# A list schedule with durations from the trace and a lock for the port that DVE and POOL share, and one count moved from ACT to DVE

## The chip, the cores and the metric

The kernel runs on one core of one Trainium2 chip. The metric is the device time of one execution in microseconds (us); the kernel before takes 649.95 us in the median of three runs (649.72 to 651.6). The engines are PE (TensorE, matrix products), DVE (VectorE), ACT (ScalarE), POOL (GpSimd) and SP, which here only issues DMAs. Each engine works through its own queue strictly in order, and an instruction that waits holds up everything behind it on its engine.

## The reference

One layer of a hybrid trunk on a sequence of 1024 tokens and 1024 channels:

```
h = rmsnorm(x, norm_g);  z = h @ w_in              # one projection, split into 14 parts
A: causal pooling over windows 2, 4, 8, 16, per-group map, scale, gated by silu(pg)
B: score = sum_h iw_h * relu(iq_h . ik)            # 8 indexer heads of 32
   sel   = top_k(score where admissible, 256)      # per query; admissible: chunks of 64 keys
   attention of 6 heads over the selected keys, gated by silu(dg)
C: softmax(q.k/8 + F[t] - F[s], s <= t) @ v, F = cumsum(log_sigmoid(ff + bias)); 6 heads, silu(fg)
x = x + concat(A, B, C) @ w_out;  return rmsnorm(x, final_g)
```

## The kernel before

Each product is made of three passes in a 32-bit matmul format (high part by high part, high by low, low by high), so a projection tile is 24 matmuls (8 slices of the inner dimension, 3 passes) into one PSUM bank. Banks 0, 1 and 6 hold projections (tag `pj`), 2 and 3 scores (`s`), 4 and 5 transposes (`pt`), 6 and 7 attention outputs. A bank that is full is read twice, first by ACT (the high part, or the tanh of a gate), then by DVE (the low part, or the gate itself); only then may PE write it again.

The program is recorded first and ordered afterwards. Every operation is put down with its engine, a planned duration, what it reads and writes, and a priority (lines 111 to 142). `schedule` (line 161) then plays the program in planned time: over all engines it takes the operation that can start earliest, by priority where several can within 3 ns, and gives out the buffers in that order. The instructions are emitted in the order of the planned starts. So the planned durations (`t_act`, `t_dve`, `t_pool`, `t_mm`, lines 275 to 288) are in no instruction, but they decide the order on every queue.

In order of the program: normalization of 8 token tiles (lines 497 to 527; the one-column chain on DVE and POOL is lines 481 to 490) and the indexer's projection (462, 544 to 567); the indexer's scores of tiles 2 to 7 (line 595 the products, 599 ACT's relu, 603 and 607 the weighted sum on DVE); the channel projections of keys, queries, values and gates, with weights split on ACT and POOL (438, 439, 694, 695); the search for the 256th largest score; attention C, attention B (919 to 1008); the output projection (1122 to 1160).

The search (lines 757 to 797) finds the threshold of each query bit by bit, 32 rounds of counting for the six tiles 2 to 7 at once (tile i has (i+1)*128 columns). In a round each tile's scores are compared with the threshold and counted: tiles 5, 6, 7 by ACT (line 771, 768, 896 and 1024 columns), tiles 2, 3, 4 by DVE (line 776, 384, 512 and 640). Then DVE makes the next threshold by lines 790 (needs only the threshold), 792 (needs all six counts) and 793, on six columns; the next round starts after 793. There are 31 such decisions after the first. `finish` (lines 799 to 850) makes masks of the thresholds on DVE, starting with line 805; a tile counted by ACT takes one more count (819) and six one-column steps (826 to 834). Beside the search run the value projections (evicted by ACT 664 and DVE 665), the pool mixer (DVE 1073 to 1085, PE 1081) and the first gates of attention C (ACT 736, DVE 738, a buffer `th` of which there are two, which the pool mixer uses as well).

Of the kernel before, what the change touches and what calls it, by code (L numbers as in the profile page):

```python
# [76 lines left out]
class Op:  # L77
    __slots__ = ("eng", "fn", "dur", "pr", "seq", "deps", "bufs", "outs", "end", "left", "bytes", "lag", "tr")


class Plan:
# [29 lines left out]
    def op(self, eng, fn, dur, r=(), w=(), pr=0.0, nbytes=0, lag=0.0, tr=False):  # L111
        o = Op()
        o.eng, o.fn, o.dur, o.pr, o.seq, o.bytes, o.lag = eng, fn, dur, pr, self.seq, nbytes, lag
        o.tr = tr
        self.seq += 1
        deps, bufs = set(), set()
        for k in r:
            bufs.add(k[0] if isinstance(k, tuple) else k)
            if k in self.last_w:
                deps.add(self.last_w[k])  # L120
        for k in w:
            bufs.add(k[0] if isinstance(k, tuple) else k)
            if k in self.last_w:
                deps.add(self.last_w[k])
            deps.update(self.readers.get(k, ()))
        for k in r:
            self.readers.setdefault(k, []).append(o)
        for k in w:
            self.last_w[k] = o
            self.readers[k] = []  # L130
        deps.discard(o)
        o.deps = deps
        o.bufs = [b for b in bufs if isinstance(b, Buf)]
        for b in o.bufs:
            b.left += 1
        o.outs = []
        o.left = len(deps)
        o.end = None
        for d in deps:
            d.outs.append(o)  # L140
        self.ops.append(o)
        return o
# [20 lines left out]
    def schedule(self):  # L163
# [9 lines left out]
        was_tr = False  # L173
        while len(order) < n:
            best = None
            for e, lst in ready.items():
                cand = []
                tmin = None
                for o in lst:
                    t = free[e] + (0.085 if e == PE and was_tr and not o.tr else 0.0)  # L180
                    for d in o.deps:
                        if d.eng == e:
                            x = d.end if e in (SP, PE, ACT) else d.end + 0.13
                        else:
                            x = d.end + self.LAT[d.eng] + (self.SLACK if e == PE else 0.0) + o.lag
                        if x > t:
                            t = x
                    ok = True
# [33 lines left out]
            if e == PE:  # L222
                was_tr = o.tr
            if e == SP:
# [50 lines left out]
def t_act(n, psum=False, acc=False):  # L275
    return (0.052 if psum else 0.094) + n / 1200.0 + (0.093 if acc else 0.0)
# [10 lines left out]
def t_mm(n):  # L287
    return 0.07 if n < 0 else max(n * 0.41667e-3 + 0.003, 0.107)
# [3 lines left out]
def tile_trunk(ctx: ExitStack, tc: tile.TileContext, x, w_in, norm_g, pool_w, pool_scale,  # L292
# [76 lines left out]
    V = lambda fn, n, r, w, pr=0.0, two=False, acc=False, fast=1: P.op(DVE, fn, t_dve(n, two, acc, fast), r, w, pr)  # L369
    G = lambda fn, n, r, w, pr=0.0: P.op(POOL, fn, t_pool(n), r, w, pr)  # L370
# [107 lines left out]
    def rstd(ss, k_ss, pr, two=False):  # L478
# [7 lines left out]
        P.op(POOL, lambda: nc.gpsimd.tensor_tensor(r0(), v(), half(), op=OP.pow), 0.47, [(b, 0), k_half], [(b, 1)], pr)  # L486
# [63 lines left out]
    def rep(i, h0, n, pr):  # L550
# [5 lines left out]
            .to_broadcast([128, n, 4, 32])), n * 189 + 10, [Z[i]], [zt], pr)  # L556
# [193 lines left out]
    def search(tiles, on_act):  # L750
# [14 lines left out]
        def count(t, kt):  # L765
            for c, i in sorted(enumerate(tiles), key=lambda x: x[1] not in on_act):
                n = (i + 1) * 128
                s = (lambda: 0.0) if t is None else (lambda c=c: t()[:, c:c + 1])
                if i in on_act:
                    jk = P.new("jka", [128, n], BF)  # L770
                    A(lambda c=c, i=i, jk=jk, s=s: nc.scalar.activation(jk(), SC[i](), AF.Sign, bias=s(), scale=-1.0,  # L771
                                                                         accum_out=cn()[:, c:c + 1]), n,
                      sck(i) + kt, [jk, k("cn", c)], pr, acc=True)
# [115 lines left out]
    def unit(kind, pair, g, ks, VV):  # L889
# [6 lines left out]
        for hd in range(2):  # L896
# [11 lines left out]
            for j in range(3, -1, -1):  # L908
                t = 4 * g + j
                Ps.insert(0, [])  # L910
                for u in range(g + 1):
# [13 lines left out]
                    if dg:  # L925
# [8 lines left out]
                      [Pt, (mx, j, u)], pr, two=True)  # L934
# [106 lines left out]
    def pool_tile(m, consts):  # L1041
# [13 lines left out]
        def add(dst, src, sh, r0, r1):  # L1055
            ksrc = kv if src is v else [(src, "d"), (src, "z")]
            G(lambda: nc.gpsimd.tensor_tensor(dst()[r0:r1, 16:], src()[r0:r1, 16:], src()[r0:r1, 16 - sh:W - sh],
                                              op=OP.add), 1024, ksrc, [(dst, "d")], pr)

        def cp():  # L1060
            G(lambda: nc.gpsimd.tensor_copy(s2()[0:64, 16:], s1()[0:64, 16:]), 1600, [(s1, "d")], [(s2, "d")], pr)
# [129 lines left out]
    on_act = [5, 6, 7]  # L1191
    tiles = on_act + [2, 3, 4]
# [46 lines left out]
```

## Time and profile before

| | |
|---|---|
| median of three runs | 649.95 us |
| profiled execution: its own time, its span | 651.98 us, 650.2 us |
| PE, DVE, ACT, POOL busy | 627.8, 474.4, 425.5, 201.6 us |
| granted PE clock, mean | 0.992 of full speed |
| DMA queue of SP | 102 MB, 55.3% of 16 engines' span |

Busy times are unions of an engine's instructions in the trace. The rows of a timeline give the start in us from the beginning of the span, the time taken, the engine, the line of the kernel, the operation, what it writes and reads, and how many instructions are merged; in brackets stands the engine's idle time before it and what ended it. A matmul's end is modelled, so a busy PE is read by its starts: in the stretch 600 to 630 us, 134 matmuls fill 30.00 us.

### The profile page before, as it was taken

The page shows a single profiled execution, that of the slowest core. Times are in us where ns is not written, and L with a number is a line of the kernel's source. Part 1 is how long each engine was busy: PE and PEld are TensorE (multiplying, and loading weights), DVE is VectorE, ACT ScalarE, POOL GpSimd, SP SyncE. Part 2 cuts the span into 40 slices and gives each one's busy share as a digit, 9 for nine tenths or more (in the row PEclk, how much of TensorE's full clock was granted, in tenths as well). Part 3 has the DMA queues.
Part 4 walks back from the last instruction along what each step waited for, and adds up shares of the span by engine and source line. Part 5 has one row for each costly group of instructions (what it writes and reads, how often), then busy time and mean ns, then how long its engine had stood idle before and what let it go on. Part 6 is the DMA issues. An engine that isn't in the chain of part 4 may idle for free. (4 is left out here: it accounts for less than half of the span.)

```text
span 650.2 us, 10279 instructions
## 1 busy us (share of the span) xinstructions
PE 627.8 (97%) x3280; PEld 529.0 (81%) x3280; DVE 474.4 (73%) x1187; ACT 425.5 (65%) x945; POOL 201.6 (31%) x218
## 2 busy tenths in 40 slices
PE   8799999999999999799999999999999999999995
PEld 7698777789988999588888888888888687788884
DVE  5987999877776887889997768766757877643322
ACT  6645678698899888513478776688477879622121
POOL 3510212450017640126252614312131625232211
PEclk9999999999999999989999999999999999999999
DMA  8616453461026337845669678599946554547311
GB/s 241 192 53 176 148 156 109 129 184 44 0 87 157 103 127 208 196 124 138 176 200 247 202 211 212 155 252 270 242 162 169 166 165 148 157 161 226 120 43 66
DMA packets 95380, 102.72 MB, mean 158 GB/s; under 512 B 8055, under 2 KB 64471, under 8 KB 95326
## 3 DMA queue, kind: packets, MB, share of 16 engines
q1 hardware_dynamic: 95326, 102.07, 55.3%
q8 instruction: 26, 0.43, 0.3%
q14 instruction: 28, 0.23, 0.1%
HBM read 72.09 MB, written 29.96 MB: 157 GB/s over the span
## 5 line engine op out<-in xcount | busy, mean ns | idle before, releaser
L462 PE MATMUL bank<-RA 128*128 128x512 f32 (+2 forms) x2016 | 481.4, 378 | 3.8 <-DVE FA L738 3.8
L462 PEld LDWEIGHTS bank<-RA 128*128 128x128 f32 x2016 | 359.7, 189 | 54.0 <-DVE FA L738 4.3
L771 ACT ACTIVATE FA<-FA 128x768 bf16<-128x768 f32 (+2 forms) x96 | 99.6, 1037 | 15.8 <-DVE FA L793 12.4
L695 POOL TENSOR_TENSOR RA<-FA,RA 128x512 fp32r<-128x512 f32 x44 | 60.2, 1382 | 145.7 <-ACT RA L694 129.4
L941 ACT ACTIVATE FA<-FA 128x512 f32<-128x512 f32 (+3 forms) x144 | 86.8, 605 | 19.2 <-DVE FA L936 19.0
L963 ACT ACTIVATE RA<-bank 128x512 fp32r<-128x512 f32 (+1 forms) x120 | 64.5, 552 | 41.5 <-PE bank L956 36.7
L930 DVE CUSTOM_DVE_ANT_0 FA<-bank,FA 128x512 f32<-128x512 f32 (+3 forms) x144 | 77.3, 550 | 19.6 <-PE bank L922 11.2
L965 DVE TENSOR_TENSOR RA<-bank,RA 128x512 fp32r<-128x512 f32 (+1 forms) x120 | 74.1, 634 | 20.2 <-ACT RA L963 18.5
L956 PE MATMUL bank<-FA 128*128 128x128 f32 x432 | 72.6, 275 | 1.0 <-ACT FA L941 1.0
L776 DVE TENSOR_SCALAR_CACHE_REDUCE FA<-FA 128x384 bf16<-128x384 f32 (+2 forms) x96 | 71.2, 742 | 1.9
L956 PEld LDWEIGHTS bank<-FA 128*128 128x128 f32 x432 | 53.6, 140 | 20.9 <-ACT FA L941 4.3
L607 DVE SCALAR_TENSOR_TENSOR FA<-FA 128x512 f32<-128x512 f32 (+3 forms) x70 | 52.8, 776 | 2.3
L919 PE MATMUL bank<-RA 128*128 128x512 f32 (+3 forms) x144 | 52.1, 362 | 0.3 <-DVE FA L930 0.2
L974 PE MATMUL bank<-RA 128*128 128x512 f32 (+3 forms) x144 | 50.1, 376 | 0.5 <-DVE RA L965 0.5
L922 PE MATMUL bank<-RA 128*128 128x512 f32 (+3 forms) x144 | 50.1, 352 | 0.0
L599 ACT ACTIVATE FA<-bank 128x512 f32<-128x512 f32 (+3 forms) x80 | 39.7, 527 | 15.1 <-PE bank L595 6.2
L926 POOL TENSOR_TENSOR FA<-FA 128x128 f32<-128x128 f32 x48 | 29.1, 610 | 65.4 <-DVE FA L930 45.5
L969 PE MATMUL bank<-RA 128*128 128x512 f32 (+3 forms) x144 | 45.4, 341 | 0.3 <-DVE FA L1003 0.3
L1123 POOL TENSOR_TENSOR RA<-FA,RA 128x1024 fp32r<-128x1024 f32 x8 | 19.2, 2399 | 46.4 <-ACT RA L1122 35.3
L1135 DVE TENSOR_TENSOR FA<-bank,FA 128x512 f32<-128x512 f32 x16 | 11.0, 687 | 30.9 <-PE bank L462 30.9
L1007 POOL TENSOR_TENSOR FA<-FA 128x512 f32<-128x512 f32 x12 | 16.1, 1348 | 56.0 <-DVE FA L1003 35.9
L919 PEld LDWEIGHTS bank<-RA 128*128 128x128 f32 x144 | 27.1, 188 | 6.2 <-DVE FA L930 2.5
(145 smaller groups left out, 689.1 us busy)
## 6 DMA issues: line engine op xcount, KB each, us to landing
FA<-in_w_in_dram SPq DMA_DIRECT2D x60, 256.0 KB, 3.8
FA<-in_x_dram SPq DMA_DIRECT2D x15, 512.0 KB, 4.1
RA<-qk_fq SPq DMA_DIRECT2D x12, 512.0 KB, 8.2
RA<-qk_dq SPq DMA_DIRECT2D x12, 512.0 KB, 11.2
RA<-qk_dk SPq DMA_DIRECT2D x18, 256.0 KB, 6.0
mix<-FA SPq DMA_DIRECT2D x16, 256.0 KB, 4.1
FA<-in_w_out_dram SPq DMA_DIRECT2D x16, 256.0 KB
FA<-mix SPq DMA_DIRECT2D x8, 512.0 KB
```

The source lines that it names most:

```text
L462: M(lambda: nc.tensor.matmul(p()[:, :n], fa(), fb(), start=st, stop=sp), n, keys, [p], pr)
L607: V(lambda rl=rl, w=w, acc=acc, wc=wc: nc.vector.scalar_tensor_tensor(acc(), rl()[:, :w], wc(), acc(), op0=OP.mult, op1=OP.add), w, [rl, ( ...
L695: G(lambda raw=raw, s=s: nc.gpsimd.tensor_tensor(Wl()[:, s, :], raw(), f32(Wh()[:, s, :]), op=OP.subtract), 512, [raw, (Wh, kh)], [(Wl, kh ...
L771: A(lambda c=c, i=i, jk=jk, s=s: nc.scalar.activation(jk(), SC[i](), AF.Sign, bias=s(), scale=-1.0, accum_out=cn()[:, c:c + 1]), n, sck(i) ...
L776: V(lambda c=c, i=i, jk=jk, s=s: nc.vector.tensor_scalar(jk(), SC[i](), s(), None, op0=OP.is_lt, op1=OP.add, accum_out=cn()[:, c:c + 1]), ...
L919: M(lambda s=s, k=k, n=n, j=j, hd=hd: nc.tensor.matmul(s()[:, :n], q()[:, hd, j * 128:j * 128 + 128], k()[:, hd, :n], start=True, stop=False),
L922: M(lambda s=s, k=k, n=n, j=j, hd=hd: nc.tensor.matmul(s()[:, :n], q()[:, 2 + hd, j * 128:j * 128 + 128], k()[:, hd, :n], start=False, sto ...
L930: V(lambda s=s, Pt=Pt, n=n, u=u, j=j, mx=mx, bias=bias: nc.vector.tensor_tensor_reduce(Pt()[:, :n], s()[:, :n], bias()[:, u * 512:u * 512 ...
L941: A(lambda Pt=Ps[j][u], n=n, j=j, u=u, hd=hd, nm=nm: nc.scalar.activation(Pt()[:, :n], Pt()[:, :n], AF.Exp, bias=nm()[:, j:j + 1], accum_o ...
L956: M(lambda pt=pt, j=j, d=d, Pt=Ps[j][kb // 4], c=kb % 4 * 128: nc.tensor.transpose(pt()[:, j * 128 - d:j * 128 - d + 128], Pt()[:, c:c + 1 ...
L963: A(lambda ph=ph, pt=pt, c=c: nc.scalar.activation(ph()[:, c], pt()[:, c], AF.Copy), n, [pt], [ph], pr, psum=True)
L965: V(lambda ph=ph, pl=pl, pt=pt, c=c: nc.vector.tensor_tensor(pl()[:, c], pt()[:, c], f32(ph()[:, c]), op=OP.subtract), n, [pt, ph], [pl], pr)
```

## The change

Three things are changed, and nothing else. First, planned durations: an accumulating ACT operation is planned 0.1 us longer (a count of the search 0.12 us more on top), a matmul 0.0105 us longer, a transpose 0.0025 us shorter, POOL's replication, additions and copy of the pool mixer shorter (lines 561, 1063, 1066 of the new kernel), its power 0.03 us longer, and attention's masked maximum (line 936 before) without the surcharge for two inputs. Second, the planner knows a lock: an operation marked `lock` is not planned to start while another marked one runs. Marked are the DVE operations recorded with `two` or `fast`, and POOL's operations recorded through `G` with more than four columns. Third, tile 5 is counted by DVE in place of ACT.

```
+                    if o.lock:
+                        t = max(t, port)
...
+            if o.lock:
+                port = t + o.dur
...
-    return (0.052 if psum else 0.094) + n / 1200.0 + (0.093 if acc else 0.0)
+    return (0.052 if psum else 0.094) + n / 1200.0 + (0.193 if acc else 0.0)
...
-    return 0.07 if n < 0 else max(n * 0.41667e-3 + 0.003, 0.107)
+    return 0.0675 if n < 0 else max(n * 0.41667e-3 + 0.0135, 0.107)
...
-    V = lambda fn, n, r, w, pr=0.0, two=False, acc=False, fast=1: P.op(DVE, fn, t_dve(n, two, acc, fast), r, w, pr)
-    G = lambda fn, n, r, w, pr=0.0: P.op(POOL, fn, t_pool(n), r, w, pr)
+    V = lambda fn, n, r, w, pr=0.0, two=False, acc=False, fast=1: P.op(DVE, fn, t_dve(n, two, acc, fast), r, w, pr,
+                                                                       lock=two or fast > 1)
+    G = lambda fn, n, r, w, pr=0.0: P.op(POOL, fn, t_pool(n), r, w, pr, lock=n > 4)
...
-                    A(lambda c=c, i=i, jk=jk, s=s: nc.scalar.activation(jk(), SC[i](), AF.Sign, bias=s(), scale=-1.0,
-                                                                         accum_out=cn()[:, c:c + 1]), n,
-                      sck(i) + kt, [jk, k("cn", c)], pr, acc=True)
+                    P.op(ACT, lambda c=c, i=i, jk=jk, s=s: nc.scalar.activation(jk(), SC[i](), AF.Sign, bias=s(), scale=-1.0,
+                                                                         accum_out=cn()[:, c:c + 1]), t_act(n, acc=True) + 0.12,
+                      sck(i) + kt, [jk, k("cn", c)], pr)
...
-                      [Pt, (mx, j, u)], pr, two=True)
+                      [Pt, (mx, j, u)], pr)
...
-    on_act = [5, 6, 7]
-    tiles = on_act + [2, 3, 4]
+    on_act = [6, 7]
+    tiles = on_act + [2, 3, 4, 5]
```

The lines of the new kernel lie up to 5 higher than those of the kernel before (776 is 781, 792 is 797, 793 is 798, 738 is 743, 736 is 741, 1081 is 1086, 919 is 924). Three places show what the new plan moves.

DVE at the end of the search, before: the last round's counts (776), the two decision steps, the first step of `finish` (805) and a step of the pool mixer (1085).

```order
L793 SCALAR_TENSOR_TENSOR FA<-FA 128x6
L776 TENSOR_SCALAR FA<-FA 128x384
L790 TENSOR_SCALAR FA<-FA 128x6
L776 TENSOR_SCALAR FA<-FA 128x512
L776 TENSOR_SCALAR FA<-FA 128x640
L1085 SCALAR_TENSOR_TENSOR FA<-bank_67,FA 128x512
L792 TENSOR_TENSOR FA<-FA 128x6
L793 SCALAR_TENSOR_TENSOR FA<-FA 128x6
L805 TENSOR_SCALAR FA<-FA 128x3
L1085 SCALAR_TENSOR_TENSOR FA<-bank_67,FA 128x512
```

The same place in the changed kernel:

```order
L798 SCALAR_TENSOR_TENSOR FA<-FA 128x6
L781 TENSOR_SCALAR FA<-FA 128x384
L795 TENSOR_SCALAR FA<-FA 128x6
L781 TENSOR_SCALAR FA<-FA 128x512
L781 TENSOR_SCALAR FA<-FA 128x640
L781 TENSOR_SCALAR FA<-FA 128x768
L797 TENSOR_TENSOR FA<-FA 128x6
L798 SCALAR_TENSOR_TENSOR FA<-FA 128x6
L743 SCALAR_TENSOR_TENSOR FA<-FA,bank_65 128x512
L810 TENSOR_SCALAR FA<-FA 128x2
```

A round has a fourth count of 768 columns, the pool mixer's steps have gone forward (they stand two rounds earlier), and the first gate's step on bank 0 (`bank_65`) follows the last decision at once.

PE where the pool mixer's second pair of products meets the gates of attention C, before (`bank_65`, `bank_66`, `bank_71` are the projection banks 0, 1 and 6, `bank_67` and `bank_68` the score banks):

```order
L462 MATMUL bank_65<-RA 128x512 x24
L462 MATMUL bank_66<-RA 128x512 x24
L919 MATMUL bank_68<-RA 128x512
L922 MATMUL bank_68<-RA 128x512
L462 MATMUL bank_71<-RA 128x512 x7
L1081 MATMUL bank_67<-FA 128x512
L462 MATMUL bank_71<-RA 128x512 x6
L1081 MATMUL bank_67<-FA 128x512
L462 MATMUL bank_71<-RA 128x512 x5
L919 MATMUL bank_67<-RA 128x384
L922 MATMUL bank_67<-RA 128x384
L462 MATMUL bank_71<-RA 128x512 x6
```

And now, to the fourth gate tile:

```order
L467 MATMUL bank_65<-RA 128x512 x12
L1086 MATMUL bank_67<-FA 128x512
L1086 MATMUL bank_68<-FA 128x512
L467 MATMUL bank_65<-RA 128x512 x12
L467 MATMUL bank_71<-RA 128x512 x8
L924 MATMUL bank_67<-RA 128x512
L927 MATMUL bank_67<-RA 128x512
L924 MATMUL bank_68<-RA 128x384
L927 MATMUL bank_68<-RA 128x384
L467 MATMUL bank_71<-RA 128x512 x16
L467 MATMUL bank_66<-RA 128x512 x24
L467 MATMUL bank_65<-RA 128x512 x24
```

The pair of products now goes into two banks and stands in the first gate tile instead of the third. In both programs the fourth gate tile (the next 24 into `bank_65`) comes after the same matmuls.

ACT at the end of the search, before:

```order
L771 ACTIVATE FA<-FA 128x768
L771 ACTIVATE FA<-FA 128x896
L771 ACTIVATE FA<-FA 128x1024
L736 ACTIVATE FA<-bank_65 128x512
L736 ACTIVATE FA<-bank_66 128x512
```

And now:

```order
L776 ACTIVATE FA<-FA 128x896
L776 ACTIVATE FA<-FA 128x1024
L776 ACTIVATE FA<-FA 128x896
L776 ACTIVATE FA<-FA 128x1024
L699 ACTIVATE RA<-FA 128x512
L741 ACTIVATE FA<-bank_65 128x512
```

The count of 768 columns is gone from each round; the first gate of attention C is still read behind the last count of the search.

## Rows read from the trace of the kernel before

**Rows 1.** The page, busy us (share of the span) and instructions.
```profile
PE 627.8 (97%) x3280; PEld 529.0 (81%) x3280; DVE 474.4 (73%) x1187; ACT 425.5 (65%) x945; POOL 201.6 (31%) x218
```

**Rows 2.** What PE waited for: us in total, times, longest us.
```profile
PE bank L462 <- DVE FA L738: 3.8, 1, 3.8
PE bank L522 <- DVE RA L527: 2.3, 2, 1.2
PE bank L595 <- ACT FA L599: 2.2, 3, 0.8
```

**Rows 3.** Timeline in the scores, from 72 us.
```profile
72.11 3.77 POOL L695 TENSOR_TENSOR RA<-FA,RA 128x512 fp32r<-128x512 f32 x2 [7.61 <-ACT RA L694]
72.30 4.79 DVE L607 SCALAR_TENSOR_TENSOR FA<-FA 128x512 f32<-128x512 f32 x4
...
77.17 0.33 PE L595 MATMUL bank<-RA 128*128 128x128 f32 x1 [0.73 <-ACT FA L599]
...
77.62 0.73 DVE L607 SCALAR_TENSOR_TENSOR FA<-FA 128x512 f32<-128x512 f32 x1
```

**Rows 4.** Timeline of an undisturbed round of the search, DVE alone.
```profile
256.17 0.17 DVE L793 SCALAR_TENSOR_TENSOR FA<-FA 128x6 int32<-128x6 int32 x1
256.37 0.61 DVE L776 TENSOR_SCALAR_CACHE_REDUCE FA<-FA 128x384 bf16<-128x384 f32 x1
...
257.82 0.88 DVE L776 TENSOR_SCALAR_CACHE_REDUCE FA<-FA 128x640 bf16<-128x640 f32 x1
...
259.94 0.17 DVE L792 TENSOR_TENSOR FA<-FA 128x6 int32<-128x6 f32 x1 [1.23 <-ACT FA L771]
260.14 0.17 DVE L793 SCALAR_TENSOR_TENSOR FA<-FA 128x6 int32<-128x6 int32 x1
```

**Rows 5.** Groups by form: count, busy us, mean ns, idle us before.
```profile
L771 ACT ACTIVATE FA<-FA 128x768 bf16<-128x768 f32 x32 | 29.8, 932 | 12.8 <-DVE FA L793 12.4 <-DVE FA L785 0.2
...
L790 DVE TENSOR_SCALAR FA<-FA 128x6 int32<-128x6 int32 x31 | 13.3, 428 | 0.0
...
L738 DVE SCALAR_TENSOR_TENSOR FA<-FA,bank 128x512 f32<-128x512 f32 x16 | 10.9, 682 | 6.6 <-ACT FA L736 6.5
...
L665 DVE TENSOR_TENSOR RA<-bank,RA 128x384 fp32r<-128x384 f32 x16 | 8.9, 555 | 3.4 <-ACT RA L664 3.3
...
L792 DVE TENSOR_TENSOR FA<-FA 128x6 int32<-128x6 f32 x31 | 7.9, 255 | 22.8 <-ACT FA L771 22.6
...
L1085 DVE SCALAR_TENSOR_TENSOR FA<-bank,FA 128x512 f32<-128x512 f32 x4 | 3.0, 748 | 0.4 <-PE bank L1081 0.4
...
L1073 DVE SCALAR_TENSOR_TENSOR FA<-FA 128x1024 f32<-128x1024 f32 x2 | 2.6, 1278 | 0.0
...
L819 DVE TENSOR_SCALAR_CACHE_REDUCE FA<-FA 128x768 bf16<-128x768 f32 x2 | 2.0, 1009 | 0.0
```

**Rows 6.** Line 793: ns min/median/max, first and last start.
```profile
L793 DVE SCALAR_TENSOR_TENSOR FA<-FA x31: 160/167/172, 133.3 to 268.5; 128x6 int32<-128x6 int32 x31
```

**Rows 7.** Timeline at 210 us, POOL and DVE.
```profile
210.10 1.29 POOL L439 TENSOR_TENSOR RA<-FA,RA 128x512 fp32r<-128x512 f32 x1
210.11 1.30 DVE L792 TENSOR_TENSOR FA<-FA 128x6 int32<-128x6 f32 x1 [2.47 <-ACT FA L771]
```

**Rows 8.** Timeline where the search ends and PE waits.
```profile
268.71 0.17 DVE L805 TENSOR_SCALAR FA<-FA 128x3 int32<-128x3 int32 x1
...
273.56 1.23 ACT L736 ACTIVATE FA<-bank 128x512 f32<-128x512 f32 x2 [5.29 <-DMA mix<-FA]
...
275.26 0.68 DVE L738 SCALAR_TENSOR_TENSOR FA<-FA,bank 128x512 f32<-128x512 f32 x1
...
275.99 15.32 PE L462 MATMUL bank<-RA 128*128 128x512 f32 x54 [3.82 <-DVE FA L738]
```

**Rows 9.** Busy time of each engine by stretch (PE, PEld, DVE, ACT, POOL), clock, DMA.
```profile
250.00:300.00 50.00, 45.57 (x191) 36.37 (x190) 42.65 (x107) 24.11 (x48) 13.23 (x11) 0.93 0.66 171
600.00:630.00 30.00, 30.00 (x134) 24.85 (x133) 9.11 (x20) 5.42 (x9) 8.71 (x6) 1.00 0.24 88
```

More of the change, by code (lines that the diff above doesn't have):

```diff
@@ L77 @@
 class Op:
-    __slots__ = ("eng", "fn", "dur", "pr", "seq", "deps", "bufs", "outs", "end", "left", "bytes", "lag", "tr")
+    __slots__ = ("eng", "fn", "dur", "pr", "seq", "deps", "bufs", "outs", "end", "left", "bytes", "lag", "tr", "lock")
 class Plan:
@@ L109, in new, with op @@
         return b
-    def op(self, eng, fn, dur, r=(), w=(), pr=0.0, nbytes=0, lag=0.0, tr=False):
+    def op(self, eng, fn, dur, r=(), w=(), pr=0.0, nbytes=0, lag=0.0, tr=False, lock=False):
         o = Op()
         o.eng, o.fn, o.dur, o.pr, o.seq, o.bytes, o.lag = eng, fn, dur, pr, self.seq, nbytes, lag
-        o.tr = tr
+        o.tr, o.lock = tr, lock
         self.seq += 1
@@ L172, in schedule @@
         n = len(self.ops)
-        was_tr = False
+        was_tr, port = False, 0.0
         while len(order) < n:
@@ L485, in rstd @@
               k_ss[1:] + [(b, 0)], [(b, 0)], pr, two=True)
-        P.op(POOL, lambda: nc.gpsimd.tensor_tensor(r0(), v(), half(), op=OP.pow), 0.47, [(b, 0), k_half], [(b, 1)], pr)
+        P.op(POOL, lambda: nc.gpsimd.tensor_tensor(r0(), v(), half(), op=OP.pow), 0.5, [(b, 0), k_half], [(b, 1)], pr)
         V(lambda: nc.vector.scalar_tensor_tensor(a(), r0(), r0(), v(), op0=OP.mult, op1=OP.mult), 1,
@@ L555, in rep @@
             Z[i]()[:, 32 * (h0 - z0):32 * (h0 - z0 + n)].rearrange("p (h b) -> p h b", b=32)[:, :, None, :]
-            .to_broadcast([128, n, 4, 32])), n * 189 + 10, [Z[i]], [zt], pr)
+            .to_broadcast([128, n, 4, 32])), 61 * n, [Z[i]], [zt], pr)
         return zt
@@ L1057, in add @@
             G(lambda: nc.gpsimd.tensor_tensor(dst()[r0:r1, 16:], src()[r0:r1, 16:], src()[r0:r1, 16 - sh:W - sh],
-                                              op=OP.add), 1024, ksrc, [(dst, "d")], pr)
+                                              op=OP.add), 800, ksrc, [(dst, "d")], pr)
         def cp():
-            G(lambda: nc.gpsimd.tensor_copy(s2()[0:64, 16:], s1()[0:64, 16:]), 1600, [(s1, "d")], [(s2, "d")], pr)
+            G(lambda: nc.gpsimd.tensor_copy(s2()[0:64, 16:], s1()[0:64, 16:]), 412, [(s1, "d")], [(s2, "d")], pr)
         add(s1, v, 1, 0, 128)
```

## The prediction

> **What bounds the kernel now.** I read the busy times first: PE is busy for 97% of the span, DVE for 73%, ACT for 65% [rows 1]. So the time is PE's own work plus the gaps in it, and a change of order can win or lose only gaps. In full flow 134 matmuls fill 30.00 us [rows 9], 0.224 us each, and nothing in the diff changes the number of matmuls. Next I read what PE waited for. One wait stands out, 3.8 us for line 738; the transposes of the normalization (522) cost 2.3, the indexer's products (595) 2.2 in three waits [rows 2]. The timeline at the large one shows its chain: ACT cannot read the first gate tile until a buffer is free (it waits 5.29 us for the pool mixer's store), DVE finishes bank 0 at 275.26 + 0.68, and PE starts the fourth gate tile at 275.99 after 3.82 us idle, so it had arrived at 272.2 [rows 8]. [...] That place is worth 3.8 + 3 = 6.8 us, and it depends on when the search ends. So the search is what I work out.
>
> **The search, step by step.** Before, a round is set by ACT: three counts, and DVE idles 1.23 us of an undisturbed round for them; from decision to decision it lasts 260.14 - 256.17 = 3.97 us [rows 4]. The change takes 32 counts of 0.93 us from ACT and gives DVE 32 of 1.01 us (by the same kind of count in line 819) [rows 5]. DVE's new round: the first three counts run from 256.37 to 257.82 + 0.88 = 258.70, that is 2.33; the fourth adds 1.01 and some 0.05 between them; line 792 to 793 is 0.20, 793 to the next count 0.20, and some 0.05 in front of 792 [rows 4]. Sum 3.84, I take 3.85. ACT's two remaining counts are far below that. So an undisturbed round is hardly shorter: 3.85 against 3.97.
>
> What changes is what else hides in it. Before, other DVE work fell into the 1.23 us of idleness; now it adds to the round. Between the first decision and the last the new order has on DVE 2 low parts of line 723 (0.68, as 738), 16 of 665 (0.555), 4 of 738 (0.682), 4 of 1085 (0.748), 2 of 1073 (1.278) and 4 steps of 16 columns (0.17, taken as a step of six) [rows 4, 5]: 1.4 + 8.9 + 2.7 + 3.0 + 2.6 + 0.7 = 19.3. Neighbours on DVE overlap a little (the accumulator's read-out, about 0.08 each), 28 x 0.08 = 2.2 off: 17.1.
>
> The third part is the port. In the row at 210.11 the decision step 792, six columns, takes 1.30 us instead of 0.17, exactly beside a POOL subtraction of 1.29 [rows 7]. Summed: 790 takes 13.3 us for 31 and 792 takes 7.9 [rows 5]; at 0.17 each they would take 5.3 and 5.3, so the excess is 8.0 + 2.6 = 10.6. Before, the 8.0 at line 790 lay mostly within DVE's idle time. In the new round it lies on the chain. [...]
>
> I charge 9 of the 10.6, since in the first three rounds ACT, with weight splits in its queue, still sets the pace. Bounds: 4 (half of the collisions happen to fall beside counts) and 16 (each of the two steps hit one and a half times as often, as POOL has more work in the denser stretch).
>
> The start: the first decision was at 133.3 [rows 6]. In the new order the indexer's scores end slightly later in PE's queue, but they should run smoother: four steps of line 607 took 4.79 us next to two POOL subtractions of 3.77, where a step alone takes 0.73, and PE waited 0.73 for it [rows 3]. These are operations the lock does cover. Of the 2.2 us at line 595 [rows 2] I take 1.0 as won (bounds: 2.2 won, 2.2 lost in new waits) and put the first decision at 132.3. This gain is not added again: PE loses it at the gate if the search is late.
>
> Last decision: 132.3 + 30 x 3.85 + 17.1 + 9 = 273.9, against 268.5 [rows 6]. Now the first gate's DVE step stands right behind it and ACT's part is done by then (two counts and 1.2 us, less than a round), so bank 0 is free at 273.9 + 0.17 + 0.68 = 274.8. The buffer that held ACT up before is free in time, since line 1085 now stands two rounds earlier. So the old wait for a store is gone, and a wait for the search takes its place. PE, which comes at about 272, goes on at 274.8 instead of 275.99: 1.2 us won. [...]
>
> **The rest.** DVE then starts `finish` at 274 instead of 268.71, with less to do: one count of 768 columns (1.01) and six one-column steps go, about 2. PE's next need of DVE, in attention's first scores, is some 25 us of matmuls away. I take 0; bounds 0 and +3, because in 250 to 300 DVE is busy 42.65 of 50 us [rows 9] and can hardly catch up. Head: the waits of the transposes (2.3, [rows 2]) depend on the same port; I take 0, bounds -2 and +2. The longer matmul in the plan only moves instructions; it takes some lead away that DVE and ACT had over the old plan, in which 24 matmuls were 0.25 us too short. In attention that can cost waits or none: 0, bounds -1 and +4.
>
> Sum: -1.2. The profiled execution would take 651.98 - 1.2 = 650.8; it lies 2.0 above the median of the runs shown, so on the median's scale 649.95 - 1.2 = 648.75. I forecast 648.8. About 0.3%, 1.95 us, is what a measurement can tell from no change.
>
> **Rivals.** All hang on the port's share p in the search, with the release at 265.8 + p.
>
> *The wait goes altogether.* If p is below 6.4, bank 0 is free before PE comes at 272.2, PE does not idle, and the clock does not fall: 3.8 + 3 = 6.8 won, 643. For it: DVE's undisturbed round is a little shorter, POOL's work comes in bursts, and the exclusion in the plan spaces part of it. Against it: the excess of 10.6 was paid already.
>
> *The search ends later, and the change is slower.* From p = 12.2 on the release lies over 1.95 us behind the old 275.99. At p = 16 it is 281.8, so +5.8: 655.8. Its place is lines 790 and 792 between the counts on DVE, its price each 1.3 us of POOL. For it: before, ACT's queue and DVE's idle time took the collisions; now nothing does, and the lock does not see these operations. Against it: the same number of POOL operations.
>
> *The cushion in attention is lost.* The plan's PE is 5% slower now, while ACT's and DVE's evictions stay planned short (738 is planned at 0.605 and takes 0.682 [rows 5]). If one in ten of the 144 score tiles makes PE wait for 0.3 us, this is +4.3: 654. Against it: PE waits of attention hardly show among the longest [rows 2].
>
> *The lock does nothing.* Where planned exclusion only reorders, the scores' 1.0 is not won; +1.0 on the sum, 649.8, within no change.
>
> **Chances.** The forecast's own case (p from 6.4 to 12.2, with the small terms within 3 either way) gets 0.42: of it 0.13 fall under 648.0, 0.22 within 1.95 of the old time, 0.07 above. The wait gone 0.25, all faster. The late search 0.22, slower. The lost cushion 0.06, slower. The idle lock 0.05, same. Faster 0.38, same 0.27, slower 0.35. The forecast's own range is 646 to 652. The range for 8 in 10 reaches into the cases on both sides: 641.5 (6.8 won and the scores' or the head's 1.5) to 656.
>
> **What would show it.** Right: rounds of about 3.85 plus what stands in them, with DVE hardly idle between 130 and 270; long rows of 790 and 792 beside POOL; the last decision at 274 (within 3); PE's largest wait still at the fourth gate tile, behind line 738 and now directly behind the search, with no wait of ACT for a store; four steps of 607 nearer to 2.9 us. Wrong: DVE idle in the search, so that ACT still sets the round; the wait at another place; or waits spread over attention.

## The result and the profile after

The changed kernel takes 656.94 us in the median of four runs (654.84 to 660.06), the kernel before 649.84 on the same chip: a ratio of 1.0111, with a 95% interval of 1.0062 to 1.0161. It is slower by 7.1 us, and outside my range of 641.5 to 656. The execution profiled below took 660.06 us, 3.1 above the median, with a span of 658.3.

The page of the changed kernel, to set against [rows 1]:

```profile
PE 629.9 (96%) x3280; PEld 529.5 (80%) x3280; DVE 502.5 (76%) x1243; ACT 394.1 (60%) x881; POOL 200.1 (30%) x218
```

What PE waited for (us in total, times, longest us), against [rows 2]:

```profile
PE bank L924 <- DVE FA L795: 5.1, 1, 5.1
PE bank L467 <- DVE RA L670: 3.3, 3, 2.5
PE bank L924 <- DVE FA L935: 3.3, 3, 2.3
PE bank L600 <- ACT FA L604: 1.7, 3, 1.2
```

DVE works 28 us more and ACT 31 less, as the moved counts ask. The wait at the gate [rows 2, 8] is gone; three others stand instead, behind the value projection's low part (670, which was 665), at attention's first products (924, which was 919) and at its third score tile.

The search: its last decision step by line, against [rows 6].

```profile
L798 DVE SCALAR_TENSOR_TENSOR FA<-FA x31: 155/167/1230, 132.8 to 277.5; 128x6 int32<-128x6 int32 x31
```

The three decision steps as groups (count, busy us, mean ns, idle us before), against [rows 5].

```profile
L797 DVE TENSOR_TENSOR FA<-FA 128x6 int32<-128x6 f32 x31 | 11.1, 359 | 2.8 <-ACT FA L776 0.5
...
L798 DVE SCALAR_TENSOR_TENSOR FA<-FA 128x6 int32<-128x6 int32 x31 | 10.4, 335 | 0.9
...
L795 DVE TENSOR_SCALAR FA<-FA 128x6 int32<-128x6 int32 x31 | 9.3, 300 | 0.0
```

Busy time by stretch (PE, PEld, DVE, ACT, POOL, clock, DMA share, GB/s); the second row answers to [rows 9].

```profile
133.00:278.00 145.00, 136.60 (x666) 121.76 (x665) 138.79 (x363) 92.36 (x167) 38.55 (x30) 0.96 0.39 112
...
250.00:300.00 50.00, 44.35 (x188) 36.02 (x188) 48.84 (x116) 22.21 (x39) 7.81 (x6) 0.93 0.61 174
```

The search ends 9.0 us later than before (277.5 against 268.5), and DVE is busy for 138.8 of its 145 us. The three steps take 30.8 us; at 0.167 for each of 93 they would take 15.5, so 15.3 are lost. They are lost beside POOL: 18 of the 93 steps took more than 0.2 us, each while a POOL instruction ran, and the others took 0.15 to 0.17. By line, 795 lost 4.1, 797 lost 6.0 and 798 lost 5.2.

What a busy DVE does to PE is seen first at 227 us (timeline; PE, ACT and DVE rows):

```profile
226.83 0.47 ACT L669 ACTIVATE RA<-bank 128x384 fp32r<-128x384 f32 x1
...
227.12 0.88 DVE L781 TENSOR_SCALAR_CACHE_REDUCE FA<-FA 128x640 bf16<-128x640 f32 x1
...
228.05 1.01 DVE L781 TENSOR_SCALAR_CACHE_REDUCE FA<-FA 128x768 bf16<-128x768 f32 x1
...
229.25 0.55 DVE L670 TENSOR_TENSOR RA<-bank,RA 128x384 fp32r<-128x384 f32 x1
...
229.86 0.47 PE L467 MATMUL bank<-RA 128*128 128x384 f32 x1 [2.47 <-DVE RA L670]
```

ACT has read the bank at 227.30, but in DVE's queue two counts and a decision step stand ahead of the low part, so the bank is free at 229.80 and PE has idled 2.47 us. Behind the wait the granted clock is 0.50 of full from 231 to 233 us. Over the 16 tiles of the value projection DVE's part begins 1.5 us after ACT's is done, in the mean; before the change it was 0.3. The last one starts at 263.2 instead of 253.7. The stores of these tiles and the loads behind them follow (timeline of SP's queue and PE):

```profile
251.16 8.76 SPq L369 DMA_DIRECT2D vd<-RA  x3
...
259.96 1.30 SPq L369 DMA_DIRECT2D RA<-qk_fk  x2
261.36 1.23 SPq L369 DMA_DIRECT2D RA<-qk_fq  x2
...
269.91 0.76 PE L924 MATMUL bank<-RA 128*128 128x512 f32 x1 [5.14 <-DVE FA L795]
```

Three stores, two of which wait for the low parts of line 670, hold SP's queue from 251.16 to 259.92, and attention's first keys and queries are asked for only then. DVE's line 795, named as releaser, had long been done; what ended the wait is the load of q, issued in two parts from 261.36, of which the second landed at 269.77 (from 255 to 275 us loads of q land 7.3 us after their issue, in the median of four). The clock falls here too (busy time by stretch, as above; the last but two is the granted clock):

```profile
270.00:275.00 5.00, 5.00 (x14) 4.04 (x15) 4.72 (x14) 3.45 (x7) 0.00 (x0) 0.55 1.06 330
```

Only 14 matmuls fall in these 5 us, where 22 fit at 0.227 us each. Then the end of the search and of `finish` (timeline; POOL and DVE, with PE's wait in the last row):

```profile
276.16 2.55 POOL L700 TENSOR_TENSOR RA<-FA,RA 128x512 fp32r<-128x512 f32 x2 [33.70 <-ACT RA L699]
...
276.53 0.95 DVE L797 TENSOR_TENSOR FA<-FA 128x6 int32<-128x6 f32 x1
277.52 1.21 DVE L798 SCALAR_TENSOR_TENSOR FA<-FA 128x6 int32<-128x6 int32 x1
278.65 0.68 DVE L743 SCALAR_TENSOR_TENSOR FA<-FA,bank 128x512 f32<-128x512 f32 x1
...
305.27 1.28 DVE L824 TENSOR_SCALAR_CACHE_REDUCE FA<-FA 128x1024 bf16<-128x1024 f32 x1
...
306.47 0.69 DVE L935 CUSTOM_DVE_ANT_0 FA<-bank,FA 128x512 f32<-128x512 f32 x1
...
307.22 0.39 PE L924 MATMUL bank<-RA 128*128 128x256 f32 x1 [2.34 <-DVE FA L935]
```

To add such places up I took, from the starts of all matmuls, the time from each start to the next, less what the same shape takes in full flow (0.227 us for 512 columns). This excess holds waits and lower clock alike. It is 35.3 us before and 43.3 after, and 8.0 is the difference of the two spans to 0.1. By stretch, to 225 us, from 225 to 300 and behind 300: 11.7, 8.2 and 15.4 before; 9.4, 13.5 and 20.4 after. So the head and the scores gained 2.3, the search's end lost 5.3 and attention 5.0, of which 4.8 lie between 300 and 325 us. Of the 5.3, 4.9 lie before 250 us, where PE waits for the low parts; from 250 to 300 the new wait for the load costs about what the old one at the gate did (0.4 more). Of the gain most lies in the head: PE's waits before 60 us fall from 6.1 to 4.2, those of line 595 only from 2.2 to 1.7.

### The profile page after: what moved, and what is told of

Same layout as the page of the kernel before. It is cut to its first block, busy times and chain, and to the rows that moved or that the text cites. A ratio compares the mean times of both kernels' runs of the same rounds, so it can differ in the third digit from the quotient of the medians.

```text
span 658.3 us, 10244 instructions
## 1 busy us (share of the span) xinstructions
PE 629.9 (96%) x3280; PEld 529.5 (80%) x3280; DVE 502.5 (76%) x1243; ACT 394.1 (60%) x881; POOL 200.1 (30%) x218
## 5 line engine op out<-in xcount | busy, mean ns | idle before, releaser
L781 DVE TENSOR_SCALAR_CACHE_REDUCE FA<-FA 128x384 bf16<-128x384 f32 (+3 forms) x128 | 103.6, 809 | 2.7
L776 ACT ACTIVATE FA<-FA 128x896 bf16<-128x896 f32 x64 | 69.9, 1092 | 54.6 <-DVE FA L798 51.5
L924 PE MATMUL bank<-RA 128*128 128x512 f32 (+3 forms) x144 | 53.1, 370 | 9.8 <-DVE FA L795 5.1
L927 PE MATMUL bank<-RA 128*128 128x512 f32 (+3 forms) x144 | 51.2, 359 | 0.0
L979 PE MATMUL bank<-RA 128*128 128x512 f32 (+3 forms) x144 | 50.3, 376 | 0.7 <-DVE RA L970 0.7
L612 DVE SCALAR_TENSOR_TENSOR FA<-FA 128x512 f32<-128x512 f32 (+3 forms) x70 | 49.7, 751 | 0.8
L974 PE MATMUL bank<-RA 128*128 128x512 f32 (+3 forms) x144 | 45.2, 340 | 1.3 <-DMA RA<-vd 1.3
L699 ACT ACTIVATE RA<-FA 128x512 fp32r<-128x512 f32 x44 | 26.9, 630 | 9.8 <-PE bank L467 9.6
L1012 POOL TENSOR_TENSOR FA<-FA 128x512 f32<-128x512 f32 x12 | 15.5, 1295 | 51.6 <-PE bank L467 21.6
```

The source lines that it names most:

```text
L776: P.op(ACT, lambda c=c, i=i, jk=jk, s=s: nc.scalar.activation(jk(), SC[i](), AF.Sign, bias=s(), scale=-1.0, accum_out=cn()[:, c:c + 1]), t ...
L781: V(lambda c=c, i=i, jk=jk, s=s: nc.vector.tensor_scalar(jk(), SC[i](), s(), None, op0=OP.is_lt, op1=OP.add, accum_out=cn()[:, c:c + 1]), ...
L924: M(lambda s=s, k=k, n=n, j=j, hd=hd: nc.tensor.matmul(s()[:, :n], q()[:, hd, j * 128:j * 128 + 128], k()[:, hd, :n], start=True, stop=False),
L927: M(lambda s=s, k=k, n=n, j=j, hd=hd: nc.tensor.matmul(s()[:, :n], q()[:, 2 + hd, j * 128:j * 128 + 128], k()[:, hd, :n], start=False, sto ...
L979: M(lambda o=o, v=v, pl=pl, c=c, j0=j0, kb=kb, nkb=nkb: nc.tensor.matmul(o()[:, j0 * 128:], v(kb), pl()[:, c], start=False, stop=(kb == nk ...
```

## The experiments

All times are medians with the ratio to the kernel before on the same chip. A profile is one execution; its excess is good to some 3 us (the changed kernel was profiled 3.1 above its median, f5 4.6 below, the others within 2.1).

| run | us | ratio, 95% interval | last decision | excess to 225, to 300, behind |
|---|---|---|---|---|
| e1_tile5_alone | 655.69 | 1.0089, 1.0069 to 1.0108 | 276.5 | 11.6, 10.8, 14.5 |
| e2_plan_alone | 654.20 | 1.0071, 1.0048 to 1.0094 | 281.8 | 7.3, 2.3, 26.2 |
| e3_short_count | 646.22 | 0.9936, 0.9916 to 0.9956 | 266.4 | 10.4, 5.1, 14.1 |
| e4_pool_memset | 646.64 | 0.9944, 0.9925 to 0.9962 | 269.5 | 6.6, 9.5, 14.7 |
| f1_old_matmul | 668.25 | 1.0266, 1.0243 to 1.0288 | 285.5 | 8.4, 7.4, 34.2 |
| f2_plan_old_matmul | 669.26 | 1.0266, 1.0237 to 1.0296 | 293.5 | 9.1, 0.2, 43.7 |
| f5_dve_durations | 680.84 | 1.0451, 1.0424 to 1.0478 | 291.7 | 7.4, 4.7, 47.8 |
| f8_control | 659.54 | 1.0135, 1.0107 to 1.0162 | 274.6 | 12.1, 14.4, 17.1 |
| g3_control_after | 657.96 | 1.0086, 1.0054 to 1.0118 | 278.5 | 11.5, 10.9, 20.2 |
| g1_order_after_act | 657.54 | 1.0085, 1.0059 to 1.0110 | 277.3 | 11.3, 12.0, 18.5 |
| g2_order_before_dve | 667.00 | 1.0238, 1.0210 to 1.0266 | 286.2 | 15.6, 21.8, 14.9 |
| h1_tile2_act | 662.77 | 1.0175, 1.0149 to 1.0201 | 279.3 | 11.2, 13.0, 23.6 |
| g1_own_scratch | 655.64 | 1.0074, 1.0051 to 1.0097 | 273.7 | 9.7, 10.0, 19.3 |
| g2_own_scratch | 659.42 | 1.0141, 1.0113 to 1.0168 | 278.9 | 12.0, 18.1, 14.3 |
| h1_own_scratch | 658.17 | 1.0115, 1.0088 to 1.0141 | 274.6 | 9.6, 11.0, 22.0 |
| h2_own_scratch | 658.32 | 1.0127, 1.0098 to 1.0157 | 274.0 | 9.1, 11.7, 20.6 |
| k1_first_scores_later | 658.07 | 1.0110, 1.0094 to 1.0126 | 277.5 | 9.0, 13.9, 18.6 |
| k2_both_later | 656.46 | 1.0089, 1.0072 to 1.0106 | 277.0 | 9.1, 13.7, 15.3 |

### Each part alone, and the changed order with less to do

e1 is the kernel before with tile 5 on DVE; e2 the changed kernel with the opposite edit.

```diff
-    on_act = [5, 6, 7]
-    tiles = on_act + [2, 3, 4]
+    on_act = [6, 7]
+    tiles = on_act + [2, 3, 4, 5]
```

> The kernel before with one edit: the counts of tile 5 on DVE; the plan's durations and its port are those of before. Search theory (32 counts of 1.01 us make DVE the pace of the search; whatever else DVE does between 133 and 278 us then adds to it, and PE waits for DVE's low parts of the value projection and for the first loads of attention): about 657 us (653 to 660), last decision at 277 (274 to 281), PE waits for line 665 or for the first products of attention together over 4 us. Plan theory (the moved count is harmless; the new durations and the port reorder the queues and cost it): 650 us (648 to 652). Port theory (what costs is only the one-row decision steps held up beside POOL): slower than the changed kernel by some us, since nothing in this plan keeps POOL and DVE apart: 658 to 662, with over 16 us of excess in lines 790, 792 and 793 against 15 in the changed kernel.

> The changed kernel with one edit: the counts of tile 5 back on ACT; new durations and port stay. Search theory: 648 us (645 to 651), last decision at 268 (266 to 271), rounds set by ACT again, PE's wait for the gate's low part back (2 to 4 us) and no wait of 5 us at the first products of attention. Plan theory: 656 us (653 to 660), with PE's waits at the first products of attention as in the changed kernel. Port theory: between them, 650 to 653.

Both are slower. e1 came as the search theory said, with the last decision at 276.5 and PE waiting for the load of q. e2's time lies where the plan theory had it, but not its waits: none at attention's first products, several of 1 to 2 us behind 300 us. What PE waited for, e1 first, then e2:

```profile
PE bank L919 <- DMA RA<-qk_fq: 4.4, 1, 4.4
PE bank L462 <- DVE FA L738: 3.0, 1, 3.0
```

```profile
PE bank L924 <- DVE FA L935: 5.5, 5, 2.1
PE bank L467 <- POOL RA L1128: 1.7, 1, 1.7
...
PE bank L990 <- DVE RA L970: 1.6, 1, 1.6
```

In e2 the search ends at 281.8, later than in the changed kernel, and PE's excess from 225 to 300 us is only 2.3: a late end costs nothing where the order has other work for PE. Its loss is in attention, 26.2 against 15.4. The parts alone (5.4 and 4.0) make 9.4 against 7.1 for both, which the intervals don't tell apart.

e3 and e4 keep every queue's order of the changed kernel.

```diff
- e3: nc.vector.tensor_scalar(jk(), SC[i](), ...
+ e3: nc.vector.tensor_scalar(jk()[:, :m], SC[i]()[:, :m], ...   # m = 128 if i == 5 else n
- e4: nc.gpsimd.tensor_tensor(Wl()[:, s, :], raw(), f32(Wh()[:, s, :]), op=OP.subtract)
+ e4: nc.gpsimd.memset(f32(Wl()[:, s, :]), 0.0)
```

> The changed kernel, every queue in the same order; tile 5 is counted over 128 of its 768 columns, with a threshold to match (640 columns of its count are left out, the rest of its selection follows another threshold). That takes some 0.55 to 0.65 us from each of 32 rounds on DVE, 18 to 21 us of the search. Search theory: last decision at 260 (256 to 266), no wait of PE over 1.5 us between 225 and 275, 649 us (646 to 651.5). Port theory: the same number of decision steps meets POOL, so lines 795, 797 and 798 keep 12 us or more of excess over 0.167 us each, the search ends only about 12 us earlier and the time is 652 to 655. Plan theory: 656 us as in the changed kernel.

> The changed kernel, every queue in the same order; POOL's subtraction that makes the low part of the projections' weights (line 700, 512 columns of two inputs) is a memset to zero, so these low parts are left out and POOL reads nothing there. Port theory: the excess of lines 795, 797 and 798 falls from 15 us to under 5, the last decision comes at 267 (264 to 270), and the time is 649 to 651. Search theory: the excess falls too, but it is only a part of what made the search late; with rounds of 3.9 us and DVE's other work still in them the last decision comes at 268 to 272 and PE still waits in part: 651 to 654. Plan theory: 656.

Both fall by about 10.5 us, under the kernel before; e4 is faster than any of its three theories said. In e3 (timeline) the low part at 228 now starts 0.04 us after ACT's step, and PE waits nowhere for line 670:

```profile
227.84 0.47 ACT L669 ACTIVATE RA<-bank 128x384 fp32r<-128x384 f32 x1
228.35 0.56 DVE L670 TENSOR_TENSOR RA<-bank,RA 128x384 fp32r<-128x384 f32 x1 [0.15 <-ACT RA L669]
```

The port theory's number for e3 (652 to 655) did not come: its decision steps keep 15.1 us of excess, and it gains all the same. e4 takes only 5.2 us out of that excess (15.3 to 10.1) and ends the search 8.0 earlier, but PE's wait of 5.1 us at line 924 stays; much of its gain is before 225 and behind 300. Its edit shortens POOL as well (44 subtractions of 1.37 us become memsets of 0.53, which need not wait for ACT), so it does not single out the collisions. e3 does single out DVE's load: in this order 20 us less of counts win 10.7 us.

### New durations, true durations and a control

Each is a change in the planner's numbers alone (f2 has tile 5 on ACT too).

```diff
- f1, f2 (from the changed kernel): max(n * 0.41667e-3 + 0.0135, 0.107)
+ f1, f2: max(n * 0.41667e-3 + 0.003, 0.107)          # transposes 0.07
- f5 (from the changed kernel): (0.13 if two else 0.07) + n / 960.0 / fast + ...
+ f5: 0.15 + n / 960.0 / fast + ...
- f8 (from the kernel before): n * 0.41667e-3 + 0.003
+ f8: n * 0.41667e-3 + 0.004
- g3 (from the changed kernel): n * 0.41667e-3 + 0.0135
+ g3: n * 0.41667e-3 + 0.0145
```

> The changed kernel with the plan's matmul time as before (0.003 us in place of 0.0135 us over the columns); all else as changed. Theory A (two separate prices: tile 5 on DVE makes DVE late between 225 and 275 us, and the longer matmul takes lead away from DVE and ACT in attention): the first price stays and the second goes: 654 us (652 to 656), PE's excess over its own pace 12 to 15 us between 225 and 300 us, and 14 to 16 us after 300. Theory B (only DVE in the search costs): 657 as in the changed kernel. Theory C (every new set of durations draws another plan, and its time scatters by some us whatever is changed): anything from 650 to 658, with waits at other places.

> The changed kernel with tile 5 on ACT again and the plan's matmul time as before; the port and the other durations stay. Theory A: 645 us (643 to 648), no wait over 2 us between 225 and 300 us, and 14 to 17 us of excess after 300 in place of the 26 of the kernel with the longer matmul. Theory C: 648 to 656, with an excess after 300 of 20 us or more at other places. A theory that the port or ACT's longer times spoil attention: 653 to 655.

> The changed kernel with one edit in the plan: DVE's time is 0.15 us over its columns instead of 0.07 or 0.13 (the traces have 0.16 to 0.17 us for six columns, 0.68 for 512 from a bank, 1.01 for a count of 768); the instructions are the same in number and kind. Theory A in its sharper form (PE waits at 227 and 264 us because the plan thinks a round of the search some 0.5 us shorter than it is, so that DVE is later than planned when PE needs it): with true times the value projection's low parts and the loads behind them come in time, or PE's other work is put ahead of them: 650 us (647 to 653), PE's excess between 225 and 300 us under 8 us in place of 13.5. If DVE is simply too full there, no plan helps: 656 (653 to 659), excess 12 or more.

> The kernel before with 0.001 us more for each matmul in the plan, 0.2 us in a thousand, a change that means nothing on the chip. Theory C: its time differs from that of before by 2 us or more, as the others do, since another plan is drawn. Theory A: within 2 us of before, 648 to 652, with PE's excess within 3 us in each of the three parts (to 225, 225 to 300, after 300).

> The changed kernel with 0.001 us more for each matmul in the plan, the control for the changed kernel as there is one for the kernel before. Scatter theory (any new number draws another order, and the order's time scatters by some us to 20): between 645 and 675, most likely 3 us or more away from the changed kernel's 657, with PE's waits at other places. Theory that the scatter is a matter of the old numbers only: 655 to 659.

Theory A fell here, and with it every account that gives a planned duration its own price. f1, f2 and f5 are slower than any theory's range. One thousandth of a microsecond more for a planned matmul makes the kernel before 8.8 us slower: PE's queue is another from its 179th matmul on. Its waits (f8):

```profile
PE bank L522 <- DVE RA L527: 3.7, 2, 2.4
PE bank L919 <- DMA RA<-qk_fq: 3.5, 1, 3.5
PE bank L462 <- DVE FA L738: 3.4, 1, 3.4
PE bank L919 <- DVE FA L930: 1.7, 3, 1.0
```

They are of the kinds seen already, at places where another order lets PE run into DVE or a load. Truer times for DVE cure the stretch they were meant for (4.7 in place of 13.5) and lose 27 us behind 300; the waits of f5 begin with

```profile
PE bank L961 <- DVE RA L970: 5.5, 8, 1.5
PE bank L974 <- DVE FA L1008: 3.7, 1, 3.7
```

g3 stayed within 2 us of the changed kernel, though its queues are another order too, so not every new draw scatters. But the changed kernel and all seven other orders drawn anew (e1, e2, f1, f2, f5, f8, g3) are slower than the kernel before, 654 to 681 us.

### One order, one count on the other engine

To price the count without a new draw, the plan was left as it is, and only the instruction in the count's place was given to the other engine. g1: changed order, tile 5 by ACT; g2: order of before, tile 5 by DVE; h1 and h2: changed order, tile 2 or 3 by ACT, with the seven steps that repair ties in `finish`.

```diff
+ if i == 5: nc.scalar.activation(junk("jka", jk), SC[i](), AF.Sign, bias=s(), scale=-1.0, accum_out=...)    # g1; h1, h2: i == 2, 3
+ if i == 5: nc.vector.tensor_scalar(junk("jkv", jk), SC[i](), s(), None, op0=OP.is_lt, op1=OP.add, ...)     # g2
```

The first three runs wrote to the planned buffer, `jk()`, which the other engine uses as well:

> The changed kernel with each queue in the changed kernel's order, but in the place of each of tile 5's 32 counts the count is done by ACT (the repair of ties for tile 5 is left out). So the plan is not drawn again; only the engine differs. Load theory (DVE, full from 133 to 278 us, is late in this order, and that costs PE's waits at 227, 264 and 304 us): 646 us (643 to 649), last decision near 268, PE's excess between 225 and 300 us 4 to 7 us in place of 13.5. Order theory (the order of the queues itself costs, whichever engine counts): 655 to 658. With ACT as the pace of the search (three counts, 3.97 us a round) it may come between, 650, with PE waiting behind ACT.

> The kernel before with each queue in its own order, but tile 5's 32 counts are done by DVE in the same places (the steps that repair ties stay as for ACT). Load theory: 656 us (653 to 660), as with the plan drawn again for it (655.7), last decision at 276 or later, PE waits for the value projection's low parts, for the first loads of attention or for the gate together 5 us more than before. Order theory: 650 (648 to 652).

> The changed kernel with each queue in the changed kernel's order, but the 32 counts of tile 2 (384 columns, 0.61 us each on DVE) are done by ACT, which idles in each round, and the steps that repair ties are added for tile 2; nothing is left out. Load theory: DVE's round falls from 3.9 to about 3.3 us, ACT's three counts take about 3.5, as much taken from DVE as by the short count of tile 5 (0.6 us a round): 646 us (644 to 649), faster than the kernel before, last decision at 264 to 268. Order theory: 655 to 658.

Each round waited for that buffer (shortest rounds 3.82, 4.49 and 3.98 us), so they decide nothing. With scratch of its own:

> As the run before it with the changed kernel's order and tile 5 counted by ACT, but ACT writes this count's 768 unused results into its own scratch buffer and not into DVE's. In that run tile 5's count waited 0.24 us in each round for DVE to leave the shared buffer, and DVE 1.1 us for the count. Load theory: that wait was the artefact; the search ends at 267 to 271 and the time is 648 us (645 to 651). Theory that the order is written for DVE's count (the place of ACT's evictions in its queue, behind a third count, makes them late instead): again 654 to 658, the search ending at 274 or later.

> As the run with the order of the kernel before and tile 5 counted by DVE, but DVE writes this count's unused results into its own scratch buffer. In that run a round lasted 4.49 us at least, since DVE's count waited for ACT to leave the shared buffer. Load theory: a round of 3.85 to 3.9 us, last decision at 275 to 279, 656 us (653 to 659). Theory that an order fits only the engine it was drawn for: 660 or more.

> As the run with the changed kernel's order and tile 2 counted by ACT, nothing left out, but ACT writes this count's unused results into its own scratch buffer; in that run DVE waited 0.31 us a round for it and a round lasted 3.98 us. Load theory: a round of 3.3 to 3.5 us, last decision at 264 to 268, 646 us (644 to 650), PE's excess between 225 and 300 us 4 to 7 us. Theory that an order fits only the engines it was drawn for: 654 or more.

> As the run before it in this list, but it is tile 3's count (512 columns, 0.74 us on DVE) that ACT does, in ACT's own scratch buffer, with the steps that repair ties; nothing is left out. Load theory: DVE is relieved by 0.74 us a round and ACT takes some 0.9: round 3.4 to 3.6, last decision at 264 to 270, 646 to 651 us. Theory that an order fits only the engines it was drawn for: 654 or more.

In the order of before the count on DVE costs 9.1 us (1.0141), by waits for DVE, though the longest, at the pool mixer's product (1090, which was 1081), is one that the load theory did not name; g2_own_scratch:

```profile
PE bank L1090 <- DVE FA L1094: 4.4, 1, 4.4
PE bank L462 <- DVE FA L738: 3.2, 1, 3.2
PE bank L462 <- DVE RA L665: 2.7, 1, 2.7
```

Its shortest round is 3.90 us, its last decision 278.9, and DVE's low parts begin 2.6 us behind ACT's. In the changed order the way back is worth at most little: 655.64 (1.0051 to 1.0097) against 1.0062 to 1.0161 for the changed kernel, not told apart. There DVE's low parts follow ACT's after 0.2 us, but ACT, behind three counts, has read its last bank of the value projection only at 261.1 (253.6 before), and the search ends at 273.7. Lateness has moved from DVE to ACT: in this order low parts stand ahead of decision steps, and DVE idles 8.2 us in front of them until ACT has read the bank (3.3 before). These 4.9 us more are about the 5.2 by which its search, from the first decision to the last, is longer than before (140.4 against 135.2). h1 and h2 relieve DVE as much as e3 did (its counts take 76 and 73 us of the search, 75 in e3, 95 in the changed kernel), by work given to ACT; they gain nothing. DVE now idles 17 and 20 us there behind ACT's counts and evictions (8 in e3, 0.6 in the changed kernel), so it is not DVE's load alone that counts. The load theory's numbers (648, 646 and 646 to 651) failed in all three.

### PE's waits moved

k1 and k2 keep all queues but PE's, and there move four or eight products.

```diff
+ for a, b, n in ((0, 4, 60),):                 # k1: score products 0 to 3 stand 60 PE operations later
+ for a, b, n in ((0, 4, 60), (4, 8, 20)):      # k2: and products 4 to 7 stand 20 later
```

> The changed kernel with one edit in PE's queue: attention's first four products (two score tiles, lines 924 and 927), which waited 5.14 us for the load of q and whose results DVE reads only at 306.47 us, stand 60 matmuls later; every other instruction of every queue stands where it stood. Theory that the wait for the load is the price: 5.1 us of wait and 3.4 us of half clock go, 648.5 us (646 to 651). Search theory (DVE is late, and PE pays for it wherever it next needs DVE): PE now comes to the gate tile in bank 0 some 9 us earlier, at 273 to 274 us, while line 743 frees that bank behind the last decision at about 279.3; a wait of 4 to 6 us behind line 743 takes the place of the wait for the load, with half clock behind it: 655 to 658, as the changed kernel.

> As the run before it, and attention's next four products (the third and fourth score tile), of which the first waited 2.34 us for DVE's first reduction of scores at 306.47, stand 20 matmuls later as well. If each place is paid by itself: 3 to 4 us less than the run before it (the wait of 2.3 and 1.7 of half clock): 645 by the load theory, 652 to 654 by the search theory. If DVE's backlog only moves on (the reductions of scores come no earlier, and the tiles behind wait instead): within 1.5 us of the run before it.

What the search theory said came, in time and in place. PE's timeline in k1 (its 488, 764 and 819 are 467, 743 and 798 of the changed kernel), then DVE's:

```profile
259.64 14.20 PE L488 MATMUL bank<-RA 128*128 128x512 f32 x60
279.32 6.64 PE L488 MATMUL bank<-RA 128*128 128x512 f32 x20 [5.48 <-DVE FA L764]
...
277.48 1.19 DVE L819 SCALAR_TENSOR_TENSOR FA<-FA 128x6 int32<-128x6 int32 x1
278.59 0.67 DVE L764 SCALAR_TENSOR_TENSOR FA<-FA,bank 128x512 f32<-128x512 f32 x1
```

Without the wait for q, PE comes to bank 0 at 273.8 and waits 5.48 us there for the end of the search, and the 20 matmuls behind take 6.64 us where 60 ahead of it took 14.20: 0.33 us each against 0.24. The 5.1 us were no price of the load. The second place is worth 1.6 us, between the two expectations (1.0110 to 1.0089; the intervals overlap, the four runs of each do not).

## Why the prediction was wrong

Right was what I read of the search's parts. PE's own work is unchanged. The shortest round is 3.89 us (I had 3.85), DVE sets it and hardly idles, the first decision is at 132.8 (132.3), and four steps of the weighted sum take 2.73 us (2.9). The counts paid nothing beside POOL, as in my sum, which has 1.01 us for the fourth: four of 768 columns that ran wholly within a POOL instruction of two inputs took 1.01 us at most, as alone. The 3 us that I added to the gate's wait of 3.8 are the clock's: in the trace of before the granted clock is 0.50 of full from 275.4 to 281.9 us, at the end of that wait and behind it, and the 54 matmuls behind it [rows 8] take about 3 us more than at the pace of full flow [rows 9]. That the head's waits for line 527 depend on POOL the same trace shows only in part: 490 and 487 took 1.31 and 1.33 us beside POOL at 22.95 and 24.18, but 527 itself took 0.69 at 19.44, wholly beside a POOL subtraction, as everywhere. The gain ahead of the search came near mine by luck: I took 1.0 at the scores and nothing in the head, and 0.5 and 1.9 of waits went.

The step that failed first is "Last decision: 132.3 + 30 x 3.85 + 17.1 + 9 = 273.9". It was 277.5; with the measured start the same sum leaves 12.1 for what I called the port in place of 9, inside my bounds of 4 and 16. No run shows a port; what the trace shows is 18 steps of 0.40 to 1.75 us beside POOL in place of 0.17. They lost more than 12.1: some 14 us up to the start of the last decision, while rounds and other work took 2.0 less than my 115.5 + 17.1. I had put this loss on lines 790 and 792 and nothing on 793, which ran undisturbed before [rows 6]; as 798 it lost 5.2 in five steps, one of them the last. With that last step held for 1.21 us, bank 0 is free at 279.3 and not at 274.8, 3.3 later than before instead of 1.2 earlier. k1 shows that wait where I had put it, behind the gate's step on DVE. This was the rival of the late search, whose condition (p from 12.2) was all but met; yet by its sum a p of 12.1 gives only 1.9 us more than before.

Second, I let a late search be paid at the gate alone. The low parts of line 665 stood in my sum as time that DVE spends, not as something PE waits for. The rows at 227 us and of SP's queue show the rest of the chain: low part, bank and store, SP's queue, load, product, with a lower clock behind each wait (0.50 of full from 231 to 233 us, 0.55 from 270 to 275). They cost 4.9 us before 250, a term that my sum had at nothing; the late end itself, paid at the load in place of the gate, added only 0.4 to what the old wait had cost. "I take 0" for `finish`, with an end of +3, was as wrong: the third score tile waits 2.34 us for DVE, and with the lower clock behind it (0.69 of full from 307.2 to 311 us) the stretch from 300 to 325 lost 4.8. These two terms make 9.7 of the loss, and the head gave some of it back.

Third, and largest in what it teaches, though it does not show where I looked for it (behind 325 us attention lost only 0.2): I priced the planner's new numbers by one term of -1 to +4 us ("only moves instructions"). A thousandth of a microsecond moves the control by 8.8 us, and truer durations for DVE move the changed kernel by some 23. No view of the profile could give that term, and I had no rival for it. Held in one order, the count costs 9.1 us in the order of before; drawn anew for it, with the old numbers, 5.4 (e1); and in the changed order some 10 us hang on it (e3). How much of the 7.1 is the moved count and how much the new numbers has no single answer, since the count's price hangs on the numbers: 5.4 us with those of before, none that shows between f1 and f2 (1.0266 both). Which of the new numbers brought what, or whether the lock did, stays open: no run has the lock by itself.

## What to carry to other kernels

Where a list schedule decides the order, measure its scatter first: change a planned time by a hair, and credit no edit with less than that moves. To price one operation, keep the drawn order and change only the instruction in its place, with its own scratch. And before a wait is called a price, move the instruction that waits: if another wait of the same length takes its place, the engine behind that one is the bound.

## What the chip showed

Beside POOL's subtraction the decision steps with two tensor inputs took 0.95 and 1.21 us (797 and 798, at 276.53 above) in place of 0.17. Each of the three steps began within a memset once in e4: 798 took 0.17 us there, 797 too, though it began only 0.07 us before the memset's end, and the step with one input (795) took 0.54, beside a memset of 0.53. e4's timeline:

```profile
129.77 0.99 POOL L700 MEMSET RA<- 128x512 f32 x2
...
129.89 0.17 DVE L798 SCALAR_TENSOR_TENSOR FA<-FA 128x6 int32<-128x6 int32 x1
...
189.64 0.53 POOL L700 MEMSET RA<- 128x512 f32 x1
...
190.10 0.17 DVE L797 TENSOR_TENSOR FA<-FA 128x6 int32<-128x6 f32 x1
...
266.30 0.53 POOL L700 MEMSET RA<- 128x512 f32 x1 [31.09 <-PE bank L467]
...
266.31 0.54 DVE L795 TENSOR_SCALAR FA<-FA 128x6 int32<-128x6 int32 x1
```

As groups, 797 and 798 fall from 11.1 and 10.4 us to 8.2 and 7.2 with the memset, and 795 does not (9.3 to 10.1). My prediction had rows of POOL's subtractions only, none of a memset beside these steps.
